# Batched x·yᵀ over 96 heads: pairing two heads of a group of eight instead of two rows of a group of four

## The chip, the cores and the metric

The kernel runs on one core of a Trainium2 chip. The metric is the device time of one execution in microseconds. The kernel before takes 309.21 us, the median of 3 runs that lie between 309.09 and 309.28.

A core has five engines that run side by side[...]: TensorE (matmuls; its weight loads are listed apart), VectorE, ScalarE, GpSimd and SyncE, which here issues every transfer. Sixteen DMA engines move data between the chip's large memory and the on-chip memory of 128 partitions. Matmul results go to a small accumulation memory (PSUM), from which VectorE and ScalarE copy them out. Such a copy is called an eviction below.

## What is computed

```python
# x, y: (batch 8, heads 12, 512 rows, 64 channels), float32
def reference(x, y):
    return np.einsum('bhtc,bhsc->bhts', x, y).astype(np.float32)
```

For each of 96 heads the kernel forms a 512 x 512 matrix of inner products over 64 channels. The inputs are 25.17 MB together and the output is 100.66 MB.

## The kernel before

TensorE contracts over partitions, so both operands are needed with channels on partitions, while memory holds rows of 64 channels. The kernel takes four heads at a time (24 groups). Partition p of a group holds 16 consecutive rows of one head, 32 partitions for each head. It casts to bf16, transposes on TensorE, and multiplies.

```python
G = 4; Q = 32; R = 16; K = 8; NG = 24
lpool: 6 buffers (each of xs, ys)   opool: 4 buffers (ot)   pmpool: 3   ptpool: 2

def load(g):                                   # 512 KB each
    nc.sync.dma_start(ys, yv[g])
    nc.sync.dma_start(xs, xv[g])

def prepare(g, made):
    # y is cast twice over: row slot r appears side by side with itself
    yb = bpool.tile([P, R, 2, C], bf16)
    nc.gpsimd.tensor_copy(yb, ys...to_broadcast([P, R, 2, C]))
    xb = bpool.tile([P, R * C], bf16)
    nc.gpsimd.tensor_copy(xb, xs)
    if g + 6 < NG: load(g + 6)
    yield
    for half in range(2):                      # 2 x 8 transposes of 128 x 128
        for k in range(K):
            nc.tensor.transpose(pt[:, k, :], yb[:, half * K + k]..., ident)
        # copy to yT: VectorE for half 0, ScalarE for half 1
        yield
    for k in range(K):                         # 8 transposes: row slots 2k and 2k+1
        nc.tensor.transpose(pt[:, k, :], xb[:, k * P:(k + 1) * P], ident)
    nc.vector.tensor_copy(xT, pt)
    # ... cut
```

A transpose turns 128 columns into 128 partitions. A row slot has only 64 channels, so x fills both halves with two row slots, 2k in the lower 64 partitions and 2k+1 in the upper. Every row of y must meet both, so y is doubled: both halves of yT hold the same.

```python
for g in range(NG):
    steps = prepare(g + 1, made)               # drawn on between the k below
    ot = opool.tile([P, R, S], fp32)           # 4 MB of output
    edge = g == 0 or g == NG - 1
    for k in range(K):
        pm = pmpool.tile([P, 2, S], fp32)
        for h in range(G):
            for par in range(2):               # par: lower or upper half
                nc.tensor.matmul(
                    pm[h * Q:(h + 1) * Q, par, :],
                    xT[par * C:(par + 1) * C, k, h * Q:(h + 1) * Q],
                    yT[par * C:(par + 1) * C, h * S:(h + 1) * S])
        # evict pm into ot: ScalarE for even k, VectorE for odd k
        # edge groups: a store of 1 MB after every second k
    if not edge:
        nc.sync.dma_start(ov[g], ...)          # 4 MB, 32 KB for each partition
```

Each matmul uses one tile of TensorE, 64 rows by 32 columns, and eight such tiles lie side by side in the array.

Of the kernel before, what the change touches and what calls it, by code (L numbers as in the profile page):

```python
# [1 line left out]

# [5 lines left out]


@with_exitstack  # L10
def kernel(
    ctx: ExitStack,
    tc: tile.TileContext,
    x: bass.AP,
    y: bass.AP,
    out: bass.AP,
):

    nc = tc.nc
    B, H, T, C = x.shape
    _, _, S, _ = y.shape
    P = 128
    G = 4
    Q = P // G
    R = T // Q
    NG = B * H // G
    K = R // 2
    fp32 = mybir.dt.float32  # L30
    bf16 = mybir.dt.bfloat16
    assert C * 2 == P and S == T and R == 16

    xv = x.rearrange("b h t c -> (b h t c)").rearrange("(g p n) -> g p n", p=P, n=R * C)
    yv = y.rearrange("b h t c -> (b h t c)").rearrange("(g p n) -> g p n", p=P, n=R * C)
    ov = out.rearrange("b h t s -> (b h t s)").rearrange("(g p n) -> g p n", p=P, n=R * S)

    const = ctx.enter_context(tc.tile_pool(name="const", bufs=1))
    lpool = ctx.enter_context(tc.tile_pool(name="lpool", bufs=6))
    bpool = ctx.enter_context(tc.tile_pool(name="bpool", bufs=2))  # L40
    tpool = ctx.enter_context(tc.tile_pool(name="tpool", bufs=2))
    opool = ctx.enter_context(tc.tile_pool(name="opool", bufs=4))
    ptpool = ctx.enter_context(tc.tile_pool(name="ptpsum", bufs=2, space=bass.MemoryType.PSUM))
    pmpool = ctx.enter_context(tc.tile_pool(name="pmpsum", bufs=3, space=bass.MemoryType.PSUM))

    loaded = {}

    def load(g):
        xs = lpool.tile([P, R * C], fp32)
        ys = lpool.tile([P, R * C], fp32)  # L50
        nc.sync.dma_start(ys, yv[g])
        nc.sync.dma_start(xs, xv[g])
        loaded[g] = (xs, ys)

    for g in range(6):
        load(g)

    ident = const.tile([P, P], bf16)
    make_identity(nc, ident)

    def prepare(g, made):

        xs, ys = loaded.pop(g)
        yb = bpool.tile([P, R, 2, C], bf16)
        nc.gpsimd.tensor_copy(  # L65
            yb, ys.rearrange("p (r c) -> p r c", c=C).unsqueeze(2).to_broadcast([P, R, 2, C])
        )
        xb = bpool.tile([P, R * C], bf16)
        nc.gpsimd.tensor_copy(xb, xs)  # L69
        if g + 6 < NG:  # L70
            load(g + 6)
        yield
        yT = tpool.tile([P, G * Q, R], bf16)
        xT = tpool.tile([P, K, P], bf16)
        for half in range(2):
            pt = ptpool.tile([P, K, P], bf16)
            for k in range(K):
                nc.tensor.transpose(  # L78
                    pt[:, k, :], yb[:, half * K + k].rearrange("p a c -> p (a c)"), ident
                )  # L80
            dst = yT[:, :, half * K:(half + 1) * K]
            src = pt.rearrange("p k n -> p n k")
            if half == 0:
                nc.vector.tensor_copy(dst, src)  # L84
            else:
                nc.scalar.activation(dst, src, mybir.ActivationFunctionType.Copy)  # L86
            yield
        pt = ptpool.tile([P, K, P], bf16)
        for k in range(K):
            nc.tensor.transpose(pt[:, k, :], xb[:, k * P:(k + 1) * P], ident)  # L90
        nc.vector.tensor_copy(xT, pt)  # L91
        made[g] = (xT, yT.rearrange("p n k -> p (n k)"))
        yield

    made = {}
    for _ in prepare(0, made):
        pass
    for g in range(NG):
        xT, yT = made.pop(g)
        steps = prepare(g + 1, made) if g + 1 < NG else iter(())  # L100
        ot = opool.tile([P, R, S], fp32)
        edge = g == 0 or g == NG - 1
        for k in range(K):
            if k % 2 == 0:
                next(steps, None)
            pm = pmpool.tile([P, 2, S], fp32)
            for h in range(G):
                for par in range(2):
                    nc.tensor.matmul(  # L109
                        pm[h * Q:(h + 1) * Q, par, :],  # L110
                        xT[par * C:(par + 1) * C, k, h * Q:(h + 1) * Q],
                        yT[par * C:(par + 1) * C, h * S:(h + 1) * S],
                        start=True, stop=True,
                    )
            if k % 2 == 0:
                nc.scalar.activation(ot[:, 2 * k:2 * k + 2, :], pm, mybir.ActivationFunctionType.Copy)  # L116
            else:
                nc.vector.tensor_copy(ot[:, 2 * k:2 * k + 2, :], pm)  # L118
            if edge and k % 2 == 1:
                a, b = (2 * k - 2) * S, (2 * k + 2) * S  # L120
                nc.sync.dma_start(ov[g][:, a:b], ot.rearrange("p r s -> p (r s)")[:, a:b])
        if not edge:
            nc.sync.dma_start(ov[g], ot.rearrange("p r s -> p (r s)"))  # L123


# [1 line left out]
_INS = ['x', 'y']  # L127
_OUTS = [((8, 12, 512, 512), 'float32')]


# [23 lines left out]
```

## Time and profile before

The profiled execution spans 307.5 us.

| engine | busy us | share of the span | instructions |
|---|---|---|---|
| TensorE, matmul | 158.3 | 51% | 2112 |
| TensorE, weight load | 81.2 | 26% | 2112 |
| VectorE | 157.3 | 51% | 144 |
| ScalarE | 119.1 | 39% | 121 |
| GpSimd | 70.6 | 23% | 54 |

Busy time is an average over the whole span; an engine at 51% may be waiting for another through the rest or may be the pacemaker of one stretch. Which it is has to be read from the slices, the chain of work that ended last, and the waits. SyncE issues 22 stores of 4096 KB, which take a median of 36.6 us from issue to landing, 8 of 1024 KB (23.6 us), and 24 loads each of y (35.7 us) and x (27.3 us). Most of a landing time is queueing behind earlier transfers.

The same notation returns in all extracts: `out<-in` names the program's tiles, and a line such as L118 is the line of the kernel that issued the instruction.

### The profile page before, as it was taken

The numbers are of one execution on the slowest core, as the hardware profiler recorded it, in microseconds if no ns is written. First come the engines' busy times: TensorE is split into PE (matmuls) and PEld (weight loads), VectorE is DVE, ScalarE is ACT, GpSimd is POOL, SyncE is SP. The second block draws the span as 40 slices with busy tenths as digits, with TensorE's granted clock in tenths as the row PEclk, the third lists the DMA queues.
The fourth block names the chain that finished last, engine by engine and source line by source line (L and its number), as shares of the span: only waits on it lengthen the run. The fifth ranks groups of instructions, "written<-read, shape, count | busy, mean of one in ns | idle before, by whom it ended". The sixth has DMA issues, their size and how long they took to land.

```text
span 307.5 us, 4865 instructions
## 1 busy us (share of the span) xinstructions
PE 158.3 (51%) x2112; PEld 81.2 (26%) x2112; DVE 157.3 (51%) x144; ACT 119.1 (39%) x121; POOL 70.6 (23%) x54
## 2 busy tenths in 40 slices
PE   2877775483564735648447474383754854320000
PEld 2443342341322313224133241231413412000000
DVE  0599997275373643736537356373563775340000
ACT  1587856144162341623506336053261564330000
POOL 5863354132122221222212312132121000000000
PEclk9999998556655667575575755757555575555555
DMA  7999999999999999999999999999999999999970
GB/s 288 417 376 425 449 405 462 412 427 435 415 436 429 404 450 420 432 436 409 448 426 404 457 420 413 451 412 443 428 431 431 437 431 420 439 432 426 410 302 21
DMA packets 11253, 126.14 MB, mean 410 GB/s; under 512 B 1248, under 2 KB 1248, under 8 KB 7392
## 3 DMA queue, kind: packets, MB, share of 16 engines
q1 hardware_dynamic: 11232, 125.83, 96.7%
q8 instruction: 16, 0.26, 0.3%
q14 instruction: 5, 0.04, 0.0%
HBM read 25.17 MB, written 100.66 MB: 409 GB/s over the span
## 4 chain that ended last, share of the span: by engine, by line
DMA 72%; DVE 11%; PE 2%; issue 1%; ACT 1%; POOL 1%; SPq 0%; DVEq 0%; ACTq 0%
DMA out_dram<-ot 71%; DVE ot L118 8%; DVE yT L84 2%; PE pm L109 1%; DMA ys<-in_y_dram 1%; ACT ot L116 1%; DVE xT L91 1%; PE pt L78 1%; POOL yb L65 1%; PE pt L90 0%; ACT yT L86 0%; SPq L123 0%; DVEq L118 0%; ACTq L116 0%
## 5 line engine op out<-in xcount | busy, mean ns | idle before, releaser
L118 DVE COPY ot<-pm 128x1024 f32<-128x1024 f32 x96 | 114.8, 1221 | 91.0 <-DMA out_dram<-ot 77.2
L116 ACT ACTIVATE ot<-pm 128x1024 f32<-128x1024 f32 x96 | 96.0, 1023 | 143.9 <-DMA out_dram<-ot 121.2
L109 PE MATMUL pm<-yT,xT 64*32 64x512 bf16 x1536 | 98.0, 555 | 100.6 <-ACT ot L116 84.0
L109 PEld LDWEIGHTS <-xT 64*32 64x32 bf16 x1536 | 30.0, 96 | 156.2 <-issue 142.9
L65 POOL CAST yb<-ys 128x2048 bf16<-128x2048 f32 x24 | 45.5, 1896 | 96.9 <-DMA ys<-in_y_dram 79.6
L78 PE MATMUL pt<-ident,yb 128*128 128x128 bf16 x384 | 42.8, 278 | 7.2 <-POOL yb L65 6.1
L69 POOL CAST xb<-xs 128x1024 bf16<-128x1024 f32 x24 | 25.0, 1042 | 65.1 <-PE pt L90 65.1
L78 PEld LDWEIGHTS <-yb 128*128 128x128 bf16 x384 | 35.5, 131 | 15.5 <-issue 7.8
L84 DVE COPY yT<-pt 128x1024 bf16<-128x1024 bf16 x24 | 29.2, 1215 | 7.2 <-PE pt L78 7.2
L90 PE MATMUL pt<-ident,xb 128*128 128x128 bf16 x192 | 26.4, 284 | 5.6 <-ACT yT L86 4.9
L86 ACT ACTIVATE yT<-pt 128x1024 bf16<-128x1024 bf16 x24 | 24.5, 1019 | 8.6 <-PE pt L78 8.6
L91 DVE COPY xT<-pt 128x1024 bf16<-128x1024 bf16 x24 | 16.6, 690 | 17.5 <-PE pt L90 17.5
L90 PEld LDWEIGHTS <-xb 128*128 128x128 bf16 x192 | 16.9, 127 | 18.1 <-issue 18.1
L86 ACT ACT_TABLE_LOAD x1 | 1.3, 1283 | 0.7 <-PEq L138 0.7
masks.py:199 POOL TENSOR_SCALAR_AFFINE_SELECT ident<-ident 128x128 bf16<-128x128 bf16 x1 | 0.3, 294 | 0.1
masks.py:197 POOL MEMSET ident<- 128x128 bf16 x1 | 0.2, 205 | 0.3 <-POOLq L138 0.3
L138 POOL MEMSET const-float32-0.0<- 128x1 f32 x1 | 0.1, 99 | 0.2 <-issue 0.2
L138 POOL MEMSET const-bfloat16-1.0<- 128x1 bf16 x1 | 0.1, 102 | 0.0
L138 POOL MEMSET const-uint8-127<- 128x1 uint8 x1 | 0.1, 102 | 0.0
L138 POOL MEMSET const-float32-1.0<- 128x1 f32 x1 | 0.1, 99 | 0.0
## 6 DMA issues: line engine op xcount, KB each, us to landing
out_dram<-ot SPq DMA_DIRECT2D x22, 4096.0 KB, 36.6
ys<-in_y_dram SPq DMA_DIRECT2D x24, 512.0 KB, 35.7
xs<-in_x_dram SPq DMA_DIRECT2D x24, 512.0 KB, 27.3
out_dram<-ot SPq DMA_DIRECT2D x8, 1024.0 KB, 23.6
```

The costliest lines, as they stand in the source:

```text
L65: nc.gpsimd.tensor_copy(yb, ys.rearrange("p (r c) -> p r c", c=C).unsqueeze(2).to_broadcast([P, R, 2, C]))
L69: nc.gpsimd.tensor_copy(xb, xs)
L78: nc.tensor.transpose(pt[:, k, :], yb[:, half * K + k].rearrange("p a c -> p (a c)"), ident)
L84: nc.vector.tensor_copy(dst, src)
L86: nc.scalar.activation(dst, src, mybir.ActivationFunctionType.Copy)
L90: nc.tensor.transpose(pt[:, k, :], xb[:, k * P:(k + 1) * P], ident)
L91: nc.vector.tensor_copy(xT, pt)
L109: nc.tensor.matmul(pm[h * Q:(h + 1) * Q, par, :], xT[par * C:(par + 1) * C, k, h * Q:(h + 1) * Q], yT[par * C:(par + 1) * C, h * S:(h + 1) ...
L116: nc.scalar.activation(ot[:, 2 * k:2 * k + 2, :], pm, mybir.ActivationFunctionType.Copy)
L118: nc.vector.tensor_copy(ot[:, 2 * k:2 * k + 2, :], pm)
L138: nc = _bacc.Bacc("TRN2", target_bir_lowering=False, num_devices=1)
```

## The change

The new kernel takes eight heads at a time (12 groups). A load brings heads a = 0 (the first four) and a = 1 (the last four) into one tile, 1 MB. The cast puts row slot r of head h beside row slot r of head h + 4, 64 channels each, for x and for y alike. A transpose then fills both halves of the partitions with different heads: the lower half belongs to the first four heads, the upper to the last four. x and y of one head stand in the same half, so y need not be doubled. Eight heads take 32 transposes where they took 48. The matmuls of one output tile now all use one half.

The loop over k runs once for each a, so there are 24 steps of 4 MB of output as before. The stores keep their sizes. Loads are three groups ahead, as many bytes as six groups of four heads. The casts are split into halves, four to a group. The output tiles have 3 buffers where they had 4.

```diff
-    NG = B * H // G
+    NG = B * H // (2 * G)
+    AHEAD = 3
-    lpool = ctx.enter_context(tc.tile_pool(name="lpool", bufs=6))
+    lpool = ctx.enter_context(tc.tile_pool(name="lpool", bufs=AHEAD))
-    opool = ctx.enter_context(tc.tile_pool(name="opool", bufs=4))
+    opool = ctx.enter_context(tc.tile_pool(name="opool", bufs=3))
... (load)
-        xs = lpool.tile([P, R * C], fp32)
-        ys = lpool.tile([P, R * C], fp32)
+        xs = lpool.tile([P, 2, R, C], fp32)
+        ys = lpool.tile([P, 2, R, C], fp32)
... (prepare)
-        nc.gpsimd.tensor_copy(
-            yb, ys.rearrange("p (r c) -> p r c", c=C).unsqueeze(2).to_broadcast([P, R, 2, C])
-        )
-        xb = bpool.tile([P, R * C], bf16)
-        nc.gpsimd.tensor_copy(xb, xs)
-        if g + 6 < NG:
-            load(g + 6)
+        xb = bpool.tile([P, R, 2, C], bf16)
+        for s, b in ((ys, yb), (xs, xb)):
+            for half in range(2):
+                rows = slice(half * K, (half + 1) * K)
+                nc.gpsimd.tensor_copy(b[:, rows], s[:, :, rows].rearrange("p a r c -> p r a c"))
+        if g + AHEAD < NG:
+            load(g + AHEAD)
... (x: one set of 8 transposes becomes two, copied by VectorE and ScalarE)
-        pt = ptpool.tile([P, K, P], bf16)
-        for k in range(K):
-            nc.tensor.transpose(pt[:, k, :], xb[:, k * P:(k + 1) * P], ident)
-        nc.vector.tensor_copy(xT, pt)
+        for half in range(2):
+            pt = ptpool.tile([P, K, P], bf16)
+            for k in range(K):
+                nc.tensor.transpose(
+                    pt[:, k, :], xb[:, half * K + k].rearrange("p a c -> p (a c)"), ident
+                )
+            dst = xT[:, half * K:(half + 1) * K]
+            if half == 0:
+                nc.vector.tensor_copy(dst, pt)
+            else:
+                nc.scalar.activation(dst, pt, COPY)
+            yield
... (main loop)
+        for a in range(2):
+            ot = opool.tile([P, R, S], fp32)
+            edge = (g == 0 and a == 0) or (g == NG - 1 and a == 1)
+            for k in range(K):
+                if k in (0, 3, 6):
+                    next(steps, None)
+                pm = pmpool.tile([P, 2, S], fp32)
+                for two in range(2):
+                    for h in range(G):
+                        nc.tensor.matmul(
+                            pm[h * Q:(h + 1) * Q, two, :],
+                            xT[a * C:(a + 1) * C, 2 * k + two, h * Q:(h + 1) * Q],
+                            yT[a * C:(a + 1) * C, h * S:(h + 1) * S],
+                            start=True, stop=True,
+                        )
```

More of the change, by code (lines that the diff above doesn't have):

```diff
@@ L27 @@
     R = T // Q
-    NG = B * H // G
+    NG = B * H // (2 * G)
     K = R // 2
+    AHEAD = 3
     fp32 = mybir.dt.float32
     bf16 = mybir.dt.bfloat16
+    COPY = mybir.ActivationFunctionType.Copy
     assert C * 2 == P and S == T and R == 16
-    xv = x.rearrange("b h t c -> (b h t c)").rearrange("(g p n) -> g p n", p=P, n=R * C)
-    yv = y.rearrange("b h t c -> (b h t c)").rearrange("(g p n) -> g p n", p=P, n=R * C)
-    ov = out.rearrange("b h t s -> (b h t s)").rearrange("(g p n) -> g p n", p=P, n=R * S)
+    xv = x.rearrange("b h t c -> (b h t c)").rearrange("(g a p n) -> g p a n", a=2, p=P, n=R * C)
+    yv = y.rearrange("b h t c -> (b h t c)").rearrange("(g a p n) -> g p a n", a=2, p=P, n=R * C)
+    ov = out.rearrange("b h t s -> (b h t s)").rearrange("(g a p n) -> g a p n", a=2, p=P, n=R * S)
     const = ctx.enter_context(tc.tile_pool(name="const", bufs=1))
-    lpool = ctx.enter_context(tc.tile_pool(name="lpool", bufs=6))
+    lpool = ctx.enter_context(tc.tile_pool(name="lpool", bufs=AHEAD))
     bpool = ctx.enter_context(tc.tile_pool(name="bpool", bufs=2))
     tpool = ctx.enter_context(tc.tile_pool(name="tpool", bufs=2))
-    opool = ctx.enter_context(tc.tile_pool(name="opool", bufs=4))
+    opool = ctx.enter_context(tc.tile_pool(name="opool", bufs=3))
     ptpool = ctx.enter_context(tc.tile_pool(name="ptpsum", bufs=2, space=bass.MemoryType.PSUM))
@@ L48, in load @@
     def load(g):
-        xs = lpool.tile([P, R * C], fp32)
-        ys = lpool.tile([P, R * C], fp32)
-        nc.sync.dma_start(ys, yv[g])
-        nc.sync.dma_start(xs, xv[g])
+        xs = lpool.tile([P, 2, R, C], fp32)
+        ys = lpool.tile([P, 2, R, C], fp32)
+        nc.sync.dma_start(ys.rearrange("p a r c -> p a (r c)"), yv[g])
+        nc.sync.dma_start(xs.rearrange("p a r c -> p a (r c)"), xv[g])
         loaded[g] = (xs, ys)
-    for g in range(6):
+    for g in range(AHEAD):
         load(g)
@@ L64, in prepare @@
         yb = bpool.tile([P, R, 2, C], bf16)
-        nc.gpsimd.tensor_copy(
-            yb, ys.rearrange("p (r c) -> p r c", c=C).unsqueeze(2).to_broadcast([P, R, 2, C])
-        )
-        xb = bpool.tile([P, R * C], bf16)
-        nc.gpsimd.tensor_copy(xb, xs)
-        if g + 6 < NG:
-            load(g + 6)
+        xb = bpool.tile([P, R, 2, C], bf16)
[5 more added lines that the diff above has]
+            load(g + AHEAD)
         yield
         yT = tpool.tile([P, G * Q, R], bf16)
-        xT = tpool.tile([P, K, P], bf16)
+        xT = tpool.tile([P, R, P], bf16)
         for half in range(2):
@@ L85, in prepare @@
             else:
-                nc.scalar.activation(dst, src, mybir.ActivationFunctionType.Copy)
+                nc.scalar.activation(dst, src, COPY)
             yield
-        pt = ptpool.tile([P, K, P], bf16)
-        for k in range(K):
-            nc.tensor.transpose(pt[:, k, :], xb[:, k * P:(k + 1) * P], ident)
-        nc.vector.tensor_copy(xT, pt)
+        for half in range(2):
[10 more added lines that the diff above has]
+            yield
         made[g] = (xT, yT.rearrange("p n k -> p (n k)"))
-        yield
     made = {}
@@ L100 @@
         steps = prepare(g + 1, made) if g + 1 < NG else iter(())
[L101 to L121, printed above, removed]
@@ L122 @@
-        if not edge:
-            nc.sync.dma_start(ov[g], ot.rearrange("p r s -> p (r s)"))
+        for a in range(2):
+            ot = opool.tile([P, R, S], fp32)
+            otf = ot.rearrange("p r s -> p (r s)")
+            edge = (g == 0 and a == 0) or (g == NG - 1 and a == 1)
[11 more added lines that the diff above has]
+                        )
+                if k % 2 == 0:
+                    nc.scalar.activation(ot[:, 2 * k:2 * k + 2, :], pm, COPY)
+                else:
+                    nc.vector.tensor_copy(ot[:, 2 * k:2 * k + 2, :], pm)
+                if edge and k % 2 == 1:
+                    i, j = (2 * k - 2) * S, (2 * k + 2) * S
+                    nc.sync.dma_start(ov[g, a][:, i:j], otf[:, i:j])
+            if not edge:
+                nc.sync.dma_start(ov[g, a], otf)
```

## The prediction

> **What bounds the kernel now.** I read the second part of the page first, the span in 40 slices, then the DMA queues and the chain that ended last, then stretches of the last 16 us. The column order of a stretch is: start and end, its length, busy time (and count) of TensorE, its weight load, VectorE, ScalarE and GpSimd, then the granted clock, the busy share of the 16 DMA engines and GB/s.
>
> ```profile
> DMA  7999999999999999999999999999999999999970
> GB/s 288 417 376 425 449 405 462 412 427 435 415 436 429 404 450 420 432 436 409 448 426 404 457 420 413 451 412 443 428 431 431 437 431 420 439 432 426 410 302 21
> DMA packets 11253, 126.14 MB, mean 410 GB/s; under 512 B 1248, under 2 KB 1248, under 8 KB 7392
> ...
> q1 hardware_dynamic: 11232, 125.83, 96.7%
> q8 instruction: 16, 0.26, 0.3%
> ...
> DMA 72%; DVE 11%; PE 2%; issue 1%; ACT 1%; POOL 1%; SPq 0%; DVEq 0%; ACTq 0%
> ```
>
> ```profile
> 100.00:150.00 50.00, 27.63 (x344) 14.47 (x336) 25.98 (x24) 18.75 (x20) 10.74 (x8) 0.60 1.01 428
> 150.00:200.00 50.00, 28.41 (x352) 14.51 (x347) 25.96 (x24) 19.02 (x20) 11.75 (x8) 0.60 1.01 429
> 290.00:296.00 6.00, 0.00 (x0) 0.00 (x0) 0.00 (x0) 0.00 (x0) 0.00 (x0) 0.50 0.99 419
> 296.00:300.00 4.00, 0.00 (x0) 0.00 (x0) 0.00 (x0) 0.00 (x0) 0.00 (x0) 0.50 0.43 182
> 300.00:306.00 6.00, 0.00 (x0) 0.00 (x0) 0.00 (x0) 0.00 (x0) 0.00 (x0) 0.50 0.06 26
> ```
>
> The DMA engines are full from the first microseconds to 296 us, at 428 to 429 GB/s in the middle, while the busiest compute engine works 26 to 28 us of every 50. The chain agrees: 72% of the span is stores. The last line is the one to notice. A share of 0.06 is one sixteenth: from 300 to 306 us a single DMA engine is still at work. So the end is set by the slowest of 16 engines, not by their mean.
>
> The trace's packet records let me rebuild that engine's day. By size, a packet of queue 1 takes a median of 159 ns (4 KB, 6144 of them, the loads), 309 ns (8 KB, 1024, the edge stores) and 1213 ns (32 KB, 2816, the other stores). One sixteenth of each is 384 x 0.159 + 64 x 0.309 + 176 x 1.213 = 61.1 + 19.8 + 213.5 = 294.3 us. The first data packet starts at 1.8 us, so an engine with nothing else to do ends at 296.1. The increments that the last store's semaphore receives tell the rest: the eighth of its 16 comes at 298.5 us, the fifteenth at 300.1 and the sixteenth at 306.5. The gap between fifteenth and sixteenth is 0.1 us for the store that lands at 60 us, 2.0 at 149, 4.0 at 212, 6.2 at 267, and stays at 6.4 to the end. It grows in step with queue 8: eleven of its 16 packets of 16 KB start after 60 us, the last at 257.9, and 6.3 / 11 is 0.57 us for each. Sixteen KB at the rate of a 32 KB packet is 0.61 us. So I take **one DMA engine to carry the instruction fetches beside its share of the data**: 296.1 + 16 x 0.6 = 305.7, against 306.5 seen.
>
> [...] TensorE has 2112 matmuls and 2112 weight loads, 4224 / 256 = 16.5, and 16 packets of 16 KB are seen, close to each 256th instruction of TensorE. [...] the new loads alternate between two places 512 KB apart, and no trace here shows whether that matters. [...] In the kernel before, row halves alternate; afterwards all matmuls of a step share a half.
>
> **The change, part by part.**
>
> ```profile
> L118 DVE COPY ot<-pm 128x1024 f32<-128x1024 f32 x96 | 114.8, 1221 | 91.0 <-DMA out_dram<-ot 77.2
> L116 ACT ACTIVATE ot<-pm 128x1024 f32<-128x1024 f32 x96 | 96.0, 1023 | 143.9 <-DMA out_dram<-ot 121.2
> ...
> L65 POOL CAST yb<-ys 128x2048 bf16<-128x2048 f32 x24 | 45.5, 1896 | 96.9 <-DMA ys<-in_y_dram 79.6
> ...
> L69 POOL CAST xb<-xs 128x1024 bf16<-128x1024 f32 x24 | 25.0, 1042 | 65.1 <-PE pt L90 65.1
> ...
> L84 DVE COPY yT<-pt 128x1024 bf16<-128x1024 bf16 x24 | 29.2, 1215 | 7.2 <-PE pt L78 7.2
> ...
> L86 ACT ACTIVATE yT<-pt 128x1024 bf16<-128x1024 bf16 x24 | 24.5, 1019 | 8.6 <-PE pt L78 8.6
> L91 DVE COPY xT<-pt 128x1024 bf16<-128x1024 bf16 x24 | 16.6, 690 | 17.5 <-PE pt L90 17.5
> ```
>
> Columns: line, engine, operation and shapes, count, then busy us and mean ns of one, then idle time before it and who ended most of it. Both evictions idle for the stores to free an output buffer.
>
> *GpSimd:* 24 casts of 1.90 us and 24 of 1.04 (70.5 us) give way to 48 of 1024 elements; at 1.04 us, 50 us. It lies beside other work: saves nothing at the end.
>
> *Transposes and their copies:* 576 become 384. VectorE drops 12 x 1.215 + 12 x 0.69 = 22.9 us. ScalarE drops 12 x 1.02 and gains 12 copies of xT, about 1.02 each: even. Also hidden.
>
> *Matmuls:* 1536 as before, but four tiles side by side where there were eight.
>
> ```profile
> 154.74 0.63 PE L109 MATMUL pm<-yT,xT 64*32 64x512 bf16 x8
> ...
> 270.59 1.06 PE L109 MATMUL pm<-yT,xT 64*32 64x512 bf16 x16 [0.43 <-DVE ot L118]
> ```
>
> At half clock (0.50) eight matmuls took 0.63 us and sixteen 1.06, so a further set adds 0.43. One step, the 4 MB of output of four heads, now needs 16 sets of four: 16 x 0.43 = 6.9 us if they stream, 16 x 0.63 = 10.1 if each set waits for the one before. Its 16 transposes add about 2.1 us (eight took 1.05 us at the start). So TensorE needs 9.0 to 12.2 us a step at half clock, less at a higher one. VectorE needs 4 x 1.22 + (1.215 + 0.69) / 2 = 5.8 us, ScalarE 5.1. A step's traffic, 4.19 MB out and 1.05 in, takes the DMA 294.3 / 24 = 12.3 us. **Compute stays below the transfers**, at worst level with them.
>
> *Output buffers, four to three:* when a store lands and frees its buffer, two stores with their loads are still queued, 24 us of work. The next step needs 6 to 12 us before its store is issued, so the queue keeps 12 us or more. Nothing reaches the end.
>
> *Loads:* 48 transfers of 512 KB become 24 of 1 MB, in runs of 4 KB as before: the same 6144 packets, and 6.3 MB still in flight from the start. A transfer costs the engine almost nothing extra: early loads land 1.28 us apart, and eight packets of 159 ns are 1.27. So 24 fewer are worth 24 x 0.01 = 0.2 us. The first group is complete later (the first ys landed at 4.1 us; 1 MB lands near 5.4, xs near 8.0), then casts (2.1), transposes and copies; the first store leaves about 16 us instead of 14.9. By then four groups of loads, 8.4 MB, are queued, about 20 us, so the engines don't notice.
>
> *Instructions:* 192 transposes fewer, each with a weight load, are 384 instructions: 4224 falls to 3840, which is 15.0 blocks instead of 16.5. That is 14 or 15 fetches instead of 16, so 0.6 to 1.2 us less on the engine that ends last. **This is the only term on the path of any size.**
>
> Sum: -0.2 - 0.6 to -1.2, so -0.8 to -1.4. From 309.21 I choose the smaller side, because the fifteenth fetch sits just at the program's end and may well come: **308.4 us**.
>
> **The rivals.** (1) *TensorE becomes the bound.* If weight loads no longer hide and the clock stays at half, a step costs more than 12.3 us; each extra microsecond is 24 us in all. [...] against it, that the clock was 1.00 up to 50 us, when TensorE had work without pause, so a fuller TensorE should be granted more. It would show 315 to 330 us; I give it 3%. (2) *The loads slow down* because their 4 KB runs hop by 512 KB. [...] Possible, one in eight. (3) *Three buffers starve the DMA* through the order on SyncE, where a load waiting for a cast stands ahead of a finished store. Before, SyncE waited 130 us ahead of xs loads without harm, since other stores were queued; now about 12 us are in hand. One in twenty, a few microseconds. (4) *Nothing moves:* the fetches, or another engine close behind (fifteenth at 300.1), leave 309.0 to 309.4.
>
> **Range and chances.** The centre is the fetch term alone; the lower edge is the whole -1.4 plus 1.2 us for quieter DMA engines, 306.6[...]. A change over 2% would need 6.2 us either way. Below, no term comes near it: 1%. Above, only rivals 1 and a bad 3: 4%.
>
> **What would show it.** In the profile after: queue 1 at 125.83 MB with about 10,850 packets (384 small ones fewer); queue 8 with 14 or 15 packets; about 428 GB/s and a DMA share of 1.0 in the middle; the sixteenth increment of the last store 5 to 6 us behind the fifteenth, and a share of 0.06 for the last 5 us; VectorE near 134 us, GpSimd near 50, TensorE busier than 51%. Evictions should still wait for stores. I'm wrong if slices in the middle fall below 0.9, if 4 KB packets take over 165 ns, or if evictions wait mainly for TensorE.

## The result and the profile after

The changed kernel takes 307.43 us (median of 4 runs, 307.38 to 307.59), against 309.15 us for the kernel before, run beside it. The ratio is 0.9946, with a 95% interval from 0.9928 to 0.9963: 1.7 us faster, inside the range predicted, but a bigger step than the 0.8 us that the prediction's centre stood for, and bigger than the 1.4 us that all its terms come to.

The page of the changed kernel first: the busy times, the slices of the DMA engines and their rates, the queues, and the chain that ended last.

```profile
span 305.6 us, 4378 instructions
...
PE 203.8 (67%) x1920; PEld 91.5 (30%) x1920; DVE 138.4 (45%) x120; ACT 119.6 (39%) x121; POOL 49.3 (16%) x54
...
DMA  7999999999999999999999999999999999999980
GB/s 278 412 409 420 459 419 399 470 418 388 446 455 388 440 446 398 441 429 437 427 424 442 420 427 430 411 454 420 437 435 425 427 442 422 437 437 422 409 368 39
DMA packets 10867, 126.11 MB, mean 413 GB/s; under 512 B 864, under 2 KB 864, under 8 KB 7008
...
q1 hardware_dynamic: 10848, 125.83, 97.2%
q8 instruction: 15, 0.25, 0.3%
...
DMA 49%; PE 29%; DVE 5%; issue 4%; ACT 3%; POOL 1%; SPq 0%; ACTq 0%
```

The same bytes move at the same rate (430 GB/s from 100 to 150 us, 428 before), without a gap, and 384 small packets are gone. Fifteen fetches are left. Transfers hold only 49% of the chain now and TensorE 29%. That looks like a new bound and is none: a chain follows one thread of releases, and the DMA row above shows the DMA engines full while TensorE's thread ran.

The stretches, in the columns of before:

```profile
100.00:150.00 50.00, 33.93 (x327) 16.17 (x326) 23.25 (x21) 20.08 (x21) 8.10 (x8) 0.53 1.01 430
...
296.00:300.00 4.00, 0.00 (x0) 0.00 (x0) 0.00 (x0) 0.00 (x0) 0.00 (x0) 0.50 0.38 160
300.00:304.00 4.00, 0.00 (x0) 0.00 (x0) 0.00 (x0) 0.00 (x0) 0.00 (x0) 0.50 0.06 27
```

Again a single engine works at the end (0.06), and 2 us less of it: the sixteenth increment of the last store comes at 304.6 us instead of 306.5, while the fifteenth hardly moves (300.5 against 300.1). **The gain lies wholly in the engine that ends last.** The groups, and one stretch of TensorE from the timeline:

```profile
L122 PE MATMUL pm<-yT,xT 64*32 64x512 bf16 x1536 | 159.4, 586 | 67.2 <-ACT ot L129 64.7
L131 DVE COPY ot<-pm 128x1024 f32<-128x1024 f32 x96 | 117.0, 1224 | 123.0 <-DMA out_dram<-ot 63.4
L129 ACT ACTIVATE ot<-pm 128x1024 f32<-128x1024 f32 x96 | 95.9, 1023 | 115.5 <-DMA out_dram<-ot 72.1
...
L73 POOL CAST xb<-xs 128x1024 bf16<-128x1024 f32 x24 | 24.3, 1040 | 13.7 <-issue 4.9
```

```profile
140.43 5.97 PE L122 MATMUL pm<-yT,xT 64*32 64x512 bf16 x56 [8.20 <-ACT ot L129]
```

Fifty-six matmuls are 14 sets of four, and 5.97 / 14 is 0.43 us a set: they stream, and their weight loads hide (56 of them, busy for 2.26 us, within the same 5.97). Before, the same products stood as

```profile
L109 PE MATMUL pm<-yT,xT 64*32 64x512 bf16 x1536 | 98.0, 555 | 100.6 <-ACT ot L116 84.0
```

so TensorE's busy time for them rises from 98.0 to 159.4 us, and it still idles behind evictions that idle behind stores.

### The profile page after: what moved, and what is told of

It reads as the page before. It is cut to its first block, busy times and chain, and to the rows that moved or that the text cites. A ratio compares the mean times of both kernels' runs of the same rounds, so it can differ in the third digit from the quotient of the medians.

```text
span 305.6 us, 4378 instructions
## 1 busy us (share of the span) xinstructions
PE 203.8 (67%) x1920; PEld 91.5 (30%) x1920; DVE 138.4 (45%) x120; ACT 119.6 (39%) x121; POOL 49.3 (16%) x54
## 3 DMA queue, kind: packets, MB, share of 16 engines
q1 hardware_dynamic: 10848, 125.83, 97.2%
## 4 chain that ended last, share of the span: by engine, by line
DMA 49%; PE 29%; DVE 5%; issue 4%; ACT 3%; POOL 1%; SPq 0%; ACTq 0%
DMA out_dram<-ot 47%; PE pm L122 23%; DVE ot L131 5%; PE pt L95 4%; ACT ot L129 3%; PE pt L82 2%; DMA xs<-in_x_dram 2%; ACT xT L102 1%; POOL xb L73 1%; DVE xT L100 0%; SPq L55 0%; ACTq L129 0%; SPq L136 0%
## 5 line engine op out<-in xcount | busy, mean ns | idle before, releaser
L122 PE MATMUL pm<-yT,xT 64*32 64x512 bf16 x1536 | 159.4, 586 | 67.2 <-ACT ot L129 64.7
L131 DVE COPY ot<-pm 128x1024 f32<-128x1024 f32 x96 | 117.0, 1224 | 123.0 <-DMA out_dram<-ot 63.4
L122 PEld LDWEIGHTS <-xT 64*32 64x32 bf16 x1536 | 53.3, 118 | 148.1 <-issue 136.3
L73 POOL CAST yb<-ys 128x1024 bf16<-128x1024 f32 x24 | 24.3, 1040 | 143.5 <-PE pt L82 69.8
L82 PE MATMUL pt<-ident,yb 128*128 128x128 bf16 x192 | 23.9, 297 | 8.5 <-POOL yb L73 6.8
L102 ACT ACTIVATE xT<-pt 128x1024 bf16<-128x1024 bf16 x12 | 12.3, 1023 | 37.0 <-PE pt L95 30.3
L95 PEld LDWEIGHTS <-xb 128*128 128x128 bf16 x192 | 19.4, 143 | 22.7 <-issue 20.0
L82 PEld LDWEIGHTS <-yb 128*128 128x128 bf16 x192 | 19.3, 138 | 17.7 <-issue 8.2
L88 DVE COPY yT<-pt 128x1024 bf16<-128x1024 bf16 x12 | 14.6, 1216 | 8.5 <-PE pt L82 8.5
L90 ACT ACTIVATE yT<-pt 128x1024 bf16<-128x1024 bf16 x12 | 12.2, 1019 | 8.2 <-PE pt L82 8.2
L100 DVE COPY xT<-pt 128x1024 bf16<-128x1024 bf16 x12 | 8.3, 690 | 12.3 <-PE pt L95 9.8
```

Source lines behind the costliest of these rows:

```text
L73: nc.gpsimd.tensor_copy(b[:, rows], s[:, :, rows].rearrange("p a r c -> p r a c"))
L82: nc.tensor.transpose(pt[:, k, :], yb[:, half * K + k].rearrange("p a c -> p (a c)"), ident)
L90: nc.scalar.activation(dst, src, COPY)
L95: nc.tensor.transpose(pt[:, k, :], xb[:, half * K + k].rearrange("p a c -> p (a c)"), ident)
L100: nc.vector.tensor_copy(dst, pt)
L102: nc.scalar.activation(dst, pt, COPY)
```

## Experiments

The theories. A, the prediction's: instruction fetches load one DMA engine, 0.6 us each. B: the number of transfers did it. C: TensorE's own work. From the first four runs came A2: one DMA engine is slowed a little by every instruction that runs, and the fetches fall on other engines as well.

**Fewer instructions.** This kernel leaves out the products of three heads in four, and moves all bytes.

```diff
-    for h in range(G):
-        nc.tensor.matmul(pm[h * Q:(h + 1) * Q, two, :],
-            xT[a * C:(a + 1) * C, 2 * k + two, h * Q:(h + 1) * Q],
-            yT[a * C:(a + 1) * C, h * S:(h + 1) * S], ...)
+    nc.tensor.matmul(pm[:, two, :], xT[a * C:(a + 1) * C, 2 * k + two, :],
+        yT[a * C:(a + 1) * C, 0:S], ...)
```

> The changed kernel with one matmul of 64 rows by 128 columns in place of four of 64 by 32; it leaves out the products of three of the four heads (each output tile is computed against the first head's y), and moves the same bytes. TensorE has 1536 matmuls and weight loads instead of 3840, so about 6 instruction fetches instead of 15. Theory A (the fetches on one DMA engine set the end, about 0.6 us each): 9 fewer are worth 5.4 us, but the next engine ends near 300.5, so 303 to 304 us against 307.4, and the gap between the fifteenth and sixteenth increment of the last store shrinks from 4.1 us to 1 or less. Theory B (the number of transfers set the gain): no change, 307.4. Theory C (TensorE's own work matters): also faster, but with the gap of 4 us kept.

Measured: 303.12 us, ratio to the kernel before 0.9806 (0.9793 to 0.9819). The gap between the last two increments is 1.4 us. From its page:

```profile
span 301.2 us, 2074 instructions
...
PE 194.8 (65%) x768; PEld 81.8 (27%) x768; DVE 138.7 (46%) x120; ACT 119.5 (40%) x121; POOL 49.3 (16%) x54
...
q8 instruction: 6, 0.10, 0.1%
```

TensorE is busy for nearly as long as before the edit (65% against 67%). With the changed kernel's 203.8 - 159.4 = 44.4 us of transposes taken off, (194.8 - 44.4) / 384 is 0.39 us for a wide matmul, by an estimate, against 159.4 / 384 = 0.42 for a set of four. What fell is the count. C foretold a gap of 4 us and B no change, so neither explains this run; A and A2 both fit.

**More instructions, by transposes issued three times.**

```diff
-    for k in range(K):
+    for k in [q for q in range(K) for _ in range(3)]:
         nc.tensor.transpose(pt[:, k, :], ...)      # for y and for x
```

> The changed kernel with every transpose issued three times into the same place; same output. TensorE has 5376 matmuls and weight loads instead of 3840, so 6 more instruction fetches (21). Theory A: 6 x 0.6 = 3.6 us slower, 311.0, with a gap of 7 to 8 us between the last two increments. Theory B: 307.4. Theory C: slower only if TensorE becomes busy throughout, and then with evictions waiting for TensorE and the slices of DMA below 9.

Measured: 309.59 us, ratio 1.0012 (1.0005 to 1.0018), so 2.2 us above the changed kernel, with 21 fetches and a gap of 5.8 us. The direction is right, and the size falls short of A's 3.6.

**Loads of 512 KB in the changed kernel, of 1 MB in the kernel before.**

```diff
-    nc.sync.dma_start(ys.rearrange("p a r c -> p a (r c)"), yv[g])      # xs alike
+    for a in range(2):
+        nc.sync.dma_start(ys[:, a].rearrange("p r c -> p (r c)"), yv[g][:, a])
```

> The changed kernel with each 1 MB load issued as two of 512 KB, so 48 loads as in the kernel before, 24 more transfers than the changed one; nothing else differs. Theory A: 307.4 plus at most 0.3. Theory B (each transfer costs the slowest engine about 0.05 us): 308.6, and the gap between the last two increments grows by about 1 us.

```diff
-    xs = lpool.tile([P, R * C], fp32)          # ys alike; one load a group
-    nc.sync.dma_start(xs, xv[g])
+    xs = lpool.tile([P, 2, R * C], fp32)       # one load for two groups
+    nc.sync.dma_start(xs, xv[g // 2])
```

> The kernel before with the loads of two groups joined into one of 1 MB, 24 transfers fewer; TensorE keeps its 4224 matmuls and weight loads and 16 fetches. Theory A: 309.2, at most 0.3 less. Theory B: 308.0.

Measured: 307.54 us for the first (307.13 to 307.70), within the noise of the changed kernel; 308.43 us for the second, ratio 0.9975 (0.9968 to 0.9982), so 0.8 us less than the kernel before. The two don't agree on what a transfer costs: nothing in one kernel, 0.03 us in the other. B explains neither the first run nor the wide matmul. It may be part of the answer for the kernel before, where the joined loads are also issued at other times, for two groups at once; I return to it below.

**Which engine pays, packet by packet.** The records of these runs broke A. Below are the last four of the 16 increments of some transfers of the changed kernel, in us after the first increment of the same transfer.

```
landed at   last four increments     fetch between
 18.5       0.2  0.2  0.2  0.3
 22.6       0.2  0.2  0.2  1.8       19.6
 39.9       0.2  0.5  1.6  1.8       35.8
 65.3       1.6  1.7  1.9  2.8       51.2
214.8       3.4  3.8  4.7  6.2
285.2       3.3  3.7  4.7  8.8
304.6       3.3  3.7  4.7  8.8
```

The first fetch throws one engine back by 1.5 us, the second throws back another, and a third follows. So a fetch is dearer than the 0.6 us I had given it, about 1.4 us (a stop of 0.9 to 1.1, then one slow packet), but it falls on changing engines. And the engine that ends last falls behind between 214.8 and 285.2 us while the three next to it stand still. It doesn't jump, and it stops falling behind when the last eviction ends at 282 us. Its packets show how:

```
kernel                 32 KB packet          instructions that start meanwhile   stretched by
before                 239.19 to 240.49 us   32 on TensorE, 2 others             89 ns
before                 273.27 to 274.50 us   none                               14 ns
changed                250.89 to 252.16 us    31 on TensorE, 2 others             61 ns
wide matmul            247.22 to 248.47 us     7 on TensorE, 2 others             33 ns
1536 memsets (below)   66.30 to 67.60 us      0 on TensorE, 36 memsets           93 ns
```

"Stretched" is the time above the usual 1213 ns; nearly all packets of the other engines beside these keep to 1213. Theory A2 was formed here, and the next runs were made for it.

**Back to the instruction count of before.**

```diff
-    for k in range(K):
+    for k in [q for q in range(K) for _ in range(2)]:
         nc.tensor.transpose(pt[:, k, :], yb...)    # for y only
```

> The changed kernel with the transposes of y issued twice into the same place; same output. TensorE is back at 4224 matmuls and weight loads, everything else as changed. Theory A2 (formed from the first runs: the packets of one DMA engine are stretched by about 2 ns for every instruction that runs, and the fetches fall on changing engines): 384 x 2 ns, so 0.8 us slower, 308.2. Theory A (fetches on one engine, 0.6 each): one more fetch, 308.0, but in jumps. Theory B (number of transfers): 307.4. The part of the 1.7 us that this does not give back lies outside TensorE's count.

Measured: a median of 307.27 us, not 308.2. Of six runs four lie at 307.17 to 307.27 and two at 307.93 and 308.00. A2 missed by 0.9 us in the four and by 0.2 in the two: putting the instructions back cost nothing in the four and about 0.5 us in the two. A jump of 0.7 us between runs of one program says that something besides the count is in play; where the fetches fall is a candidate that I could not follow run by run.

**Instructions of another engine.**

```diff
+    for q in range(8):                          # ahead of each output tile
+        nc.gpsimd.memset(tiny[:, q:q + 1], 0.0)
```

> The changed kernel with 1536 memsets of one column of 128 partitions added on GpSimd, eight for each output tile; same output. Theory A2 for instructions of any engine: 1536 x 2 ns, about 3 us slower, 310.5, with the packets of one DMA engine stretched more. If only TensorE's instructions do it: 307.4. Theory A (TensorE's fetches alone): 307.4.

Measured: 311.06 us, ratio 1.0052 (1.0038 to 1.0067), 3.6 us above the changed kernel. From its page, the memsets' group and queue 8:

```profile
q8 instruction: 15, 0.25, 0.3%
...
L122 POOL MEMSET tiny<- 128x1 f32 x1536 | 51.6, 107 | 3.7 <-issue 3.3
```

The memsets touch 512 bytes each, and TensorE's fetches on queue 8 stay at 15. While the memsets run there are twelve 8 KB packets more of another queue, one for each 128 memsets; I take them for GpSimd's own fetches. In the records they throw back a second engine, which ends 4.6 us before the last. The last one loses the extra time without jumps, while the memsets run (to 80.4 us). Fourteen 32 KB packets in a row, from 57.9 to 77.3 us, take 2.4 us more than 14 x 1213 ns, and none is stretched by more than 249 ns. In the changed kernel fourteen packets from 55.9 to 73.7 us take 0.8 us more. **So neither TensorE's instructions nor its fetches are needed: GpSimd's instructions do it as well.**

Stretched packets are seen in every trace. What travels with an instruction to burden that DMA engine no run here tells. Each timed run was itself recorded by the profiler, so the recording may take part. A 32 KB packet moves 27 bytes in a nanosecond, so 2 ns are about 50 bytes for each instruction, by an estimate from these traces.

**Sparing the slow engine its last data.**

```diff
-    nc.sync.dma_start(ov[g, a][:, i:j], otf[:, i:j])
+    nc.sync.dma_start(ov[g, a][0:120, i:j], otf[0:120, i:j])      # last step only
+    nc.sync.dma_start(ov[g, a][120:128, i:j], otf[120:128, i:j])
```

> The changed kernel with each of the last four 1 MB stores issued as partitions 0 to 119 and partitions 120 to 127. If the 120 partitions go to 15 engines and the slow engine is the one left out, it is spared its last 9.7 us of data: the end falls to that of the others, about 300.5 plus 1.2 for what they take over, so near 304.5 by the clock of the result against 307.4. If the slow engine is among the 15: 308 to 309.

Measured: 314.95 us, ratio 1.0177 (1.0157 to 1.0197). Its stretches at the end:

```profile
300.00:306.00 6.00, 0.00 (x0) 0.00 (x0) 0.00 (x0) 0.00 (x0) 0.00 (x0) 0.50 0.20 70
306.00:312.00 6.00, 0.00 (x0) 0.00 (x0) 0.00 (x0) 0.00 (x0) 0.00 (x0) 0.50 0.06 25
```

One engine is still alone at the end, and in the records it moves eight packets and then a single one for each pair of stores: it serves the small store as well. That 120 partitions go to 15 engines was my assumption, and no run shows it. The split did not spare the slow engine, and the time lies above both expectations. It did harm: three 32 KB packets between 288 and 298 us took 3.7 to 3.9 us instead of 1.2. What made them long is not shown.

**A version with fewer instructions and the right output.**

```diff
-    xT = tpool.tile([P, R, P], bf16)
+    xT = tpool.tile([P, K, P, 2], bf16)
-    dst = xT[:, half * K:(half + 1) * K]
+    dst = xT[:, :, :, half]
-    ot = opool.tile([P, R, S], fp32)            # four heads, 32 partitions each
+    for j in range(2):                          # two heads, 64 partitions each
+        ot = opool.tile([P, K, S], fp32)
... for each row slot, i = 0, 1 and h = 2 * j + i
+        nc.tensor.matmul(pm[i * 64:(i + 1) * 64, two, :],
+            xT[a * C:(a + 1) * C, 2 * k + two, h * Q:(h + 1) * Q, :].rearrange("c q b -> c (q b)"),
+            yT[a * C:(a + 1) * C, h * S:(h + 1) * S], ...)
```

> The changed kernel with matmuls of 64 rows by 64 columns, two heads to an output tile of 64 partitions each, so that 768 matmuls do the work of 1536; the copy of xT writes every second element to bring two row slots together; stores are 2 MB in runs of 16 KB. Same output. TensorE has 2304 instead of 3840 matmuls and weight loads. Theory A2: 1536 x 2 ns = 3 us less, plus about 0.5 us if a 16 KB packet takes 0.61 us: 305.0. Theory A: 6 fewer fetches, 304.3. Theory B: 22 more transfers, 308.

Measured: 306.35 us, ratio 0.9897 (0.9881 to 0.9914). **It beats both kernels**, by 1.1 us the changed one. Its groups:

```profile
L124 PE MATMUL pm<-yT,xT 64*64 64x512 bf16 x768 | 163.2, 610 | 56.6 <-ACT ot L131 54.8
...
L100 DVE COPY xT<-pt 128x1024 bf16<-128x1024 bf16 x12 | 15.6, 1297 | 10.2 <-PE pt L95 8.8
```

The copy of xT now takes 1.30 us instead of 0.69, hidden as expected. The result is 1.3 us above what was expected, and most of that comes from the packets. A 16 KB packet takes 611 ns, so an engine has 384 x 0.159 + 32 x 0.309 + 368 x 0.611 = 295.8 us of data instead of 294.3, 1.5 us more where I had allowed 0.5. And the page counts 1414 instructions fewer, not 1536, because instructions outside TensorE were added with the smaller tiles and stores.

**The runs in one line.** With N the instructions on the first line of each page, without the split store, and with 1.5 us taken off the kernel of 64 columns for its packets, after its result was known:

| kernel | N | us | line |
|---|---|---|---|
| wide matmul | 2074 | 303.12 | 303.1 |
| 64 columns, less 1.5 | 2964 | 304.85 | 304.8 |
| changed | 4378 | 307.43 | 307.5 |
| changed, loads of 512 KB | 4426 | 307.54 | 307.6 |
| changed, y transposed twice | 4762 | 307.27 | 308.2 |
| before, loads of 1 MB | 4822 | 308.43 | 308.3 |
| before | 4865 | 309.21 | 308.4 |
| transposes three times | 5914 | 309.59 | 310.3 |
| 1536 memsets | 5914 | 311.06 | 310.3 |

The line is 299.2 us + 1.88 ns x N, a fit to the nine. Five kernels lie within 0.15 us of it and four are off by 0.7 to 0.9 us, two on each side. Against the changed kernel alone, an added memset costs 2.4 ns and an added transpose or its weight load 1.4 ns in the run with three transposes, and nothing in most runs with y transposed twice. The line is good to 0.9 us: enough for steps of 1500 instructions, and too little for one of a few hundred.

## Why the prediction was right, and where it was not

*The bound: right.* A single DMA engine sets the end in both kernels, and compute stayed off it. (The chain's 72% was all transfers; stores were 71%.) Sets of four took the 0.43 us of the better case. In the kernel before, eight matmuls side by side took 0.63 us together (from 154.74 us, at a granted clock of 0.50), where one has a median of 0.60; sixteen took 1.06 us at 0.50 (from 270.59 us) and 0.62 at 1.00 (from 14.11 us), so the same set is shorter at the higher clock. GpSimd took 49.3 us (50 foretold), queue 1 had 10,848 packets and queue 8 had 15. VectorE came to 138.4 us and not 134: the dropped copies are as computed (14.6 + 8.3 left of 29.2 + 16.6), but the evictions rose from 114.8 to 117.0, half of the difference. The last increment of the last store came 4.1 us behind the fifteenth, where 5 to 6 were foretold.

*The rivals: none came.* TensorE at 67% never held the DMA back. The reason given, that a fuller TensorE should be granted a higher clock, isn't borne out all the same: from 100 to 150 us TensorE was busy 33.9 us instead of 27.6, and the clock was 0.53 instead of 0.60; from 50 to 100 us it was busy 39.5 us instead of 28.2, at 0.65 instead of 0.58. Nor was TensorE without pause before 50 us: from 10 to 50 us it was busy 69 to 87% of the time in the kernel before. The 4 KB packets average 162.8 ns in the records after and 162.9 before, so hopping by 512 KB costs nothing measurable here; that it would slow the loads was my estimate, and no trace shows it. Three buffers kept the share at 1.00 to 1.01 from 50 to 270 us. That weight loads might no longer hide once all matmuls of a step share a half was not shown by any trace either: the four of a set shared one and streamed, at 0.43 us.

*The step that failed* is "one DMA engine to carry the instruction fetches". I read it off a lag that grew in step with queue 8. But fetches come with the instructions, one for 251 matmuls and weight loads on average in the kernel before and one for 254 in the changed one, so a lag that follows the instructions grows in step with them as well. The flat end fitted both readings too: in the kernel before the last fetch starts at 257.9 us and the last eviction ends at 272.9. What I had not looked at was whether the lag jumps or creeps, and on which engine; the records had that before any run. In place of a fetch term the runs show a lag that follows the instructions: 487 fewer (4865 to 4378), 384 of them on TensorE, which by the line is 0.9 us. That this lies within the fetch term's 0.6 to 1.2 us is luck.

*The size.* Measured 1.7 us, more than the 0.8 to 1.4 us of the prediction's sum. It is inside the range only by the 1.2 us that were allowed for quieter DMA engines. The line gives the count 0.9 us of it, but the run that puts 384 of the 487 instructions back gave up nothing in four of six cases and 0.5 us in two. Joining the loads of the kernel before brings 0.8 us, yet splitting those of the changed kernel costs nothing. My 0.2 us for 24 transfers was too small for one kernel and too large for the other. And two kernels with the same 54 loads and stores and nearly the same count, the kernel before with joined loads (4822, 308.43 us) and the changed one with y transposed twice (4762, 307.27 us), lie 1.2 us apart, of which the line explains 0.1. **So in these runs about 1 us of the 1.7 comes from something besides the count and the number of transfers, and its cause stays open.** Which engine catches which fetch, or when instructions and loads come, are candidates; no run separates them.

## What to carry to other kernels

When transfers fill the span, look at the last microseconds: a DMA share of one sixteenth (0.06 here, before and after) means that a single engine sets the end. Here what burdened it counted although the busiest compute engine worked for 51% of the span before and 67% after. Part of that burden was the number of instructions, about 2 ns each over steps of 1500 and more, TensorE's and GpSimd's alike, so fewer and larger instructions paid although the engines they ran on were waiting. Whether they pay as much when nothing is recorded has not been shown. Two causes that grow in step can't be told apart by their total; look for jumps, and change one without the other.

## What was not expected of the hardware

One DMA engine's packets lengthen while instructions run, by 61 to 93 ns of 1213 at 33 to 36 instructions a packet in the rows shown, and by 14 ns after the last eviction. A 16 KB instruction fetch stops one DMA engine for 0.9 to 1.1 us and makes its next packet slow by about 0.4, and different fetches hit different engines. That cost did not reach the end where the engine had time to spare: in the changed kernel the three engines next to the last, thrown back by fetches as well (the rows to 65.3 us), end at 300.5 us or before, against 304.6.
